# The work ahead of attention in another order: keys and queries first, natural-layout values among the first row maxima, the attention pool in two

## The chip, the core and the metric

The kernel runs on one core of one Trainium2 chip. The metric is the device time of one execution in microseconds (us); it was taken three times for the kernel before. Engines are named as in the profile: PE (TensorE, matmul; PEld is its weight load), DVE (VectorE), ACT (ScalarE), POOL (GpSimd), SP (SyncE, which issues the DMAs).

## What is computed

One transformer layer with a sequence of 1,024 tokens and a width of 1,024, in f32. Only its first third matters here:

```python
h = _rms_norm(x, norm_mix); u = h @ w_in
q, kc, vc, ks, vs, kw, vw, gate_logits, rw, merge = split(u)
# NSA attention, 8 heads of 64, 2 key groups, three branches:
#  c: compress(kc), compress(vc): blocks of 32 tokens at stride 16 -> silu -> 63 keys and values
#  s: 16 selected blocks of 64 (with 16 blocks in all: every causal token)
#  w: a window of 512 tokens
# q and the keys of each branch are rms-normed per head with a gain
o = g_c * attn_c(q) + g_s * attn_s(q) + g_w * attn_w(q)
o_rwkv = rwkv7(rw)            # token mix, low-rank ("lora") projections, a scan, group norm
x = x + (gate0 * (o @ proj_nsa) + gate1 * (o_rwkv @ proj_rwkv)) @ w_out
x = x + conv_ffn(_rms_norm(x, norm_ffn))
```

## The kernel before

Every projection is a product of f32 numbers split in a high and a low part (`hhi`, `hlo` of the normed input; `whi`, `wlo` of a weight). `wload` (L245) loads a weight of 128 output columns, splits it on ACT (L252) and DVE or POOL (L254). `passes` (L293) runs 24 matmuls of 512 columns for each half of the tokens (L264: eight `k` with `whi` by `hhi` and `hlo`, then eight with `wlo`), and calls an evacuation. So a projection of both halves is 48 matmuls.

The PSUM banks have tags: P and B for projections, A for attention scores, M for sums of squares (`RTAG`) and for the row maxima; `psM` has two banks. A scheduler orders the instructions of each engine by a priority that starts with the order of the program text; a wait for a buffer or a value moves nothing past an instruction on the same engine once the order is set.

`rms64` (L362) norms a projection per head: square on ACT (L364), a matmul with ones by blocks (L366), logarithm and exponential on ACT (L368, L369, each in its own table set), a product on DVE (L370). `kstack` (L379) writes the normed keys, as f16 high and low parts, to the stacked layouts `k1*` and `k2*` by six DMAs.

`kphase` (L390) runs once. It compresses keys (`kv` = 0) and then values (`kv` = 1): a projection, copies into `zp`, 32 small matmuls with `cw1` (L429), a SiLU that ends in `hid` (L440), a product with `cw2` (L443 for keys, L452 for values), and for the keys a norm and `kstack`. Then come the values in natural layout (tokens on partitions): one load `wn` of 128 x 2240, split in `wnh` (ACT, L461) and `wnl` (POOL, L462), and for each of eight token groups 24 matmuls of 280 columns into psA (L469), two copies and two differences into `Vs` and `Vw`, and the gates' exponential `gat` (L473 to L475). After that the mask constants `cb` are loaded (L478, into the buffer of `wn`) and cast (L479), and the keys s and w are projected, normed and stacked (L481 to L493).

`attention` (L516) calls `kphase`, opens the pool "attq" where the pool of `kphase` was, and projects the first queries (`qproj(0)`, L499). Then come eight units (four query pairs `i`, two groups `g`). Each loads `qd`, `q2` by DMA (L534 to L536), computes row maxima of branches s and w block by block (L554 and mask L558 into psM, DVE's reduction L560), of branch c (L566), turns them into shifts, and then for each branch and half computes scores (L608 to L612 into psA), two exponentials on ACT (`ph` L617, `pf` L618), a difference on DVE (`pl` L619) and the products with the values (L622 to L627 into psB). The units' written order interleaves the row maxima of the next unit with the exponentials of this one.

Fillers are woven into `attention` by `weave`, one after so many steps, from the list `FO`: numbers are `z` projections (`zproj`, L653; 48 matmuls each and stores to `z_d`), "L" is a step of `loraproj` (its inputs are the stored `z`; four steps j of three products, L980 to L986, evacuated by ACT, L989 and L992, and POOL, into the three buffers "zs" and stored to `lw_d`, `al_d`, `gt_d`, `km_d`). `z` and lora results use the same three "zs" buffers.

## Time and profile before

| | before |
|---|---|
| median of 3 runs | 1774.48 us |
| range of the runs | 1773.18 to 1779.53 us |
| the profiled execution | 1774.76 us |
| its span on the core | 1772.8 us |
| mean granted PE clock | 0.993 |
| matmul records | 11856 |

The profile is one execution. Its page gives the busy time of each engine; the windows view gives it for stretches of the span, in us from the span's start; the view of groups gives count, busy time and mean length in ns by line and shape; the timeline gives the start and length of single instructions, with idle time before them and what ended it in brackets; the view of waits gives, by pair of waiting and awaited instruction, the total in us, how often, and the longest. Matmul lengths include the pipeline, so that the distance of two starts, not the length, is what a matmul costs in a dense stream. L264 is line 264 of the kernel before.

### The profile page before, as it was taken

The page shows a single profiled execution, that of the slowest core. Times are in us where ns is not written, and L with a number is a line of the kernel's source. Part 1 is how long each engine was busy: PE and PEld are TensorE (multiplying, and loading weights), DVE is VectorE, ACT ScalarE, POOL GpSimd, SP SyncE. Part 2 cuts the span into 40 slices and gives each one's busy share as a digit, 9 for nine tenths or more (in the row PEclk, how much of TensorE's full clock was granted, in tenths as well). Part 3 has the DMA queues.
Part 4 walks back from the last instruction along what each step waited for, and adds up shares of the span by engine and source line. Part 5 has one row for each costly group of instructions (what it writes and reads, how often), then busy time and mean ns, then how long its engine had stood idle before and what let it go on. Part 6 is the DMA issues. An engine that isn't in the chain of part 4 may idle for free. (4 is left out here: it accounts for less than half of the span.)

```text
span 1772.8 us, 30784 instructions
## 1 busy us (share of the span) xinstructions
PE 1725.8 (97%) x11856; PEld 1350.3 (76%) x11856; DVE 1247.7 (70%) x2197; ACT 888.5 (50%) x1603; POOL 477.7 (27%) x346
## 2 busy tenths in 40 slices
PE   8998999999999999999999999999999999999998
PEld 5885667776777778887777878787888888888886
DVE  6425676777776548764546585499888888875799
ACT  6455674657656754446545563444444434524330
POOL 0102031110121220010013200112534444757856
PEclk9999999999999999999999999999999999999999
DMA  5325143231344445435445763444222222623302
GB/s 193 109 68 181 39 155 108 88 122 43 112 146 127 140 151 196 145 119 160 146 156 173 255 209 115 147 145 141 78 89 80 81 90 72 242 75 123 131 13 107
DMA packets 124258, 224.65 MB, mean 127 GB/s; under 512 B 16336, under 2 KB 45392, under 8 KB 123856
## 3 DMA queue, kind: packets, MB, share of 16 engines
q1 hardware_dynamic: 124112, 222.69, 38.7%
q8 instruction: 93, 1.52, 0.4%
q14 instruction: 53, 0.43, 0.1%
HBM read 153.86 MB, written 63.96 MB: 123 GB/s over the span
## 5 line engine op out<-in xcount | busy, mean ns | idle before, releaser
L264 PE MATMUL psP<-hhi,whi 128*128 128x512 f32 x560 | 229.0, 409 | 1.2 <-ACT hhi L238 0.6
L264 PE MATMUL psP<-hlo,whi 128*128 128x512 f32 x560 | 225.3, 402 | 0.0
L254 DVE TENSOR_TENSOR wlo<-wraw,whi 128x1024 fp32r<-128x1024 f32 (+1 forms) x98 | 112.0, 1144 | 76.4 <-ACT whi L252 37.4
L619 DVE TENSOR_TENSOR pl<-pf,ph 128x512 f16<-128x512 f32 (+3 forms) x208 | 117.2, 572 | 55.0 <-ACT pf L618 53.8
L264 PE MATMUL psP<-hhi,wlo 128*128 128x512 f32 x560 | 153.7, 403 | 0.0
L252 ACT ACTIVATE whi<-wraw 128x1024 fp32r<-128x1024 f32 (+1 forms) x98 | 93.0, 953 | 92.2 <-PE psP L264 41.5
L617 ACT ACTIVATE ph<-psA 128x512 f16<-128x512 f32 (+3 forms) x208 | 99.4, 478 | 66.9 <-PE psA L612 33.5
L264 PEld LDWEIGHTS psP<-hhi,whi 128*128 128x128 f32 x560 | 105.9, 189 | 26.0 <-DVE zs L659 1.2
L264 PEld LDWEIGHTS psP<-hlo,whi 128*128 128x128 f32 x560 | 105.9, 189 | 23.2 <-issue 1.4
L560 DVE TENSOR_REDUCE mp<-psM 128x1 f32<-128x512 f32 (+1 forms) x192 | 95.1, 515 | 34.9 <-PE psM L558 26.5
L264 PEld LDWEIGHTS psP<-hhi,wlo 128*128 128x128 f32 x560 | 103.0, 188 | 21.6 <-issue 0.5
L1539 POOL TENSOR_TENSOR wlo<-wraw,whi 128x1024 fp32r<-128x1024 f32 (+1 forms) x33 | 64.7, 1960 | 146.5 <-PE psA L264 46.9
L618 ACT ACTIVATE pf<-psA 128x512 f32<-128x512 f32 (+3 forms) x208 | 100.2, 482 | 0.0
L622 PEld LDWEIGHTS <-ph 128*128 128x128 f16 x592 | 55.8, 96 | 18.3 <-issue 7.8
L627 PEld LDWEIGHTS <-pl 128*128 128x128 f16 x592 | 54.9, 98 | 18.7 <-issue 6.1
L1339 POOL TENSOR_TENSOR b<-b,bonus 128x512 f32<-128x512 f32 x8 | 10.4, 1302 | 205.2 <-ACT b L1337 170.2
L641 POOL TENSOR_TENSOR onat<-onat,ot 128x256 f32<-128x256 f32 x32 | 28.3, 891 | 135.0 <-DVE ot L640 119.3
L1539 POOL TENSOR_TENSOR s34l<-s,s34h 128x1024 fp32r<-128x1024 f32 x16 | 39.2, 2450 | 93.2 <-ACT s34h L1538 93.2
L1482 DVE SCALAR_TENSOR_TENSOR th<-th,u 128x512 f32<-128x512 f32 x38 | 59.5, 1566 | 0.1
L625 PEld LDWEIGHTS <-ph 128*128 128x128 f16 x592 | 56.1, 97 | 2.4 <-issue 1.7
L1538 ACT ACTIVATE whi<-wraw 128x1024 fp32r<-128x1024 f32 (+1 forms) x38 | 33.4, 879 | 41.5 <-PE psP L1603 28.7
L1603 PE MATMUL psP<-h2h,whi 128*128 128x512 f32 x128 | 50.8, 397 | 1.2 <-ACT p L1629 1.2
(812 smaller groups left out, 5119.1 us busy)
## 6 DMA issues: line engine op xcount, KB each, us to landing
wraw<-f_up SPq DMA_DIRECT2D x56, 512.0 KB, 3.5
wraw<-w_t SPq DMA_DIRECT2D x46, 512.0 KB, 4.0
wraw<-f_dn SPq DMA_DIRECT2D x22, 512.0 KB, 4.1
th_d<-th SPq DMA_DIRECT2D x38, 256.0 KB, 2.1
sg_d<-zs SPq DMA_DIRECT2D x32, 256.0 KB, 2.4
wraw<-w_out SPq DMA_DIRECT2D x16, 512.0 KB, 3.5
z_d<-zs SPq DMA_DIRECT2D x28, 256.0 KB, 3.7
x<-xT SPq DMA_DIRECT2D x24, 256.0 KB, 5.5
```

The source lines that it names most:

```text
L252: A.activation(hi[:, :nk], raw, AF.Copy)
L254: (V if WK[0] <= wk[0] < WK[1] else G).tensor_sub(lo[:, :nk], raw, hi[:, :nk].bitcast(F32))
L264: lastm[0] = T.matmul(ps, a[:, k], ks_(b, k), start=(n == 0), stop=(n == 3 * nk - 1)).ins
L560: V.reduce_max(mp[:, x, br, t:t + 1], pm[:, 0:(b1 - b0) * 128], axis=AX.X)
L617: A.activation(ph[0:nkey, rg], pa[0:nkey, rg], AF.Exp, scale=0.125)
L618: A.activation(pf[0:nkey, rg], pa[0:nkey, rg], AF.Exp, scale=0.125)
L619: V.tensor_sub(pl[0:nkey, rg], pf[0:nkey, rg], ph[0:nkey, rg])
L622: T.matmul(pov[:, t, :], ph[0:nkey, tk], vt[0:nkey, kb, g, 0:65], start=first, stop=False, skip_group_check=True)
L625: T.matmul(pov[:, t, 0:64], ph[0:nkey, tk], vt[0:nkey, kb, g, 65:129], start=False, stop=False, skip_group_check=True)
L627: T.matmul(pov[:, t, :], pl[0:nkey, tk], vt[0:nkey, kb, g, 0:65], start=False, stop=True, skip_group_check=True)
L1482: V.scalar_tensor_tensor(th, th, 0.5, ub, op0=ALU.mult, op1=ALU.mult)
L1539: e.tensor_sub(lo[:, ks], raw[:, ks], hi[:, ks].bitcast(F32))
```

## The change

All of it is in the order of the work up to the first unit of attention, and in where the buffers lie that this order needs. Line numbers move: `rms64` is at L376 to L384 after, the row maxima's matmul at L580, the natural values' at L512, a projection's at L268, the exponentials at L650 and L651, the z evacuation at L691, the lora evacuations at L1022 and L1025.

- Both compressions run up to `hid` before either product with `cw2`; those products go to psM. The mask constants are loaded first, in four pieces on buffers of the later `prep` pool, and cast on POOL.
- The queries `q0` are projected between keys s and keys w. The norms of keys and `q0` use buffers of the `prep` pool (`ktile`). The lora weights' raw loads use these buffers too, so they are loaded behind.
- The natural-layout values become a function, `vnat`, that is emitted after the row maxima of branch w of the first unit; the matmuls of token group t are held until row maximum number 3t + 1 is issued.
- "attq" is opened first and holds queries, maxima and shifts; the pool of `kphase` is closed behind `vnat`, and a second attention pool "attp" in its place holds `onat`, `pf`, `ph`, `pl`, `cf`, `ot`, `oT`.
- Two z projections (4 and 8) trade places in `FO`.

```diff
+VPA = 3
+VPB = 1
+VAT = (0, 0, 1)
+PKT = "MM"
-FO = (12, 13, "L", 0, "L", 4, "L", 8, "L")
+FO = (12, 13, "L", 0, "L", 8, "L", 4, "L")
...
+        def ktile(x):
+            kr[0] += x == "s"
+            t_ = {"s": ("t1", "cum"), "r": ("e2", "BK"), "n": ("km", "kk")}[x][kr[0] % 2]
+            return prep.tile([128, 512], F32, name="k" + x, tag=t_, bufs=1)
...
+            cl4 = [prep.tile([128, 512], F32, name=f"cl{i}", tag=t_) for i, t_ in enumerate(("km", "kk", "t1", "cum"))]
+            for i in range(4):
...
+                load(cl4[i][:, :w_], D["cst"][:, 256 + 512 * i:256 + 512 * i + w_])
+                G.tensor_scalar(cb[:, 512 * i:512 * i + w_], cl4[i][:, :w_], 1.0, 0.0, op0=ALU.mult, op1=ALU.add)
+            z = tmp.tile([128, 2240], F32, name="zp", tag="wnl")
...
+                hids.append(hid)
+            for kv, hid in enumerate(hids):
+                if kv == 0:
+                    pk = ps(PKT[0])
...
+            for nm, br, wi, gi in (("s", 0, 2, 2), ("w", 1, 3, 3)):
+                if br:
+                    qproj(0, "A", ktile)
...
+        def vnat():
...
+            for t in range(8):
+                pn = ps("A")
...
+                for k in range(8):
+                    with tc.issue_after(pms[min(VPA * t + VPB, len(pms) - 1)]) if k == 0 and VPA else ExitStack():
                         for a, b in ((hhi, wnh), (hlo, wnh), (hhi, wnl)):
                             T.matmul(pn[:, 0:280], a[t // 4][k][:, tk], b[:, k], start=(n == 0), stop=(n == 23))
...
         def attention():
-            yield from kphase()
-            AQ["p"] = pool("attq", 1, stack=ast, side="right")
+            AQ["q"] = pool("attq", 1, stack=ast, side="right")
...
-            qproj(0, "A")
+            kst = ExitStack()
+            AQ["k"] = pool("ktmp", 1, stack=kst, side="right")
+            yield from kphase()
...
+                        if (i, g, br) == VAT:
+                            vnat()
+                            kst.close()
+                            AQ["p"] = pool("attp", 1, stack=ast, side="right")
...
+                    if g == 0:
+                        onat = AQ["p"].tile([128, 8, 128], F32, name="onat", bufs=2)
```

PE at the second compression, before: `hid` is the first compression's result, `zp_343` and `zp_344` the inputs of the convolution, `cw_349` the weight `cw2`.

```order
L264 MATMUL psP<-hhi_92,wlo 128x512
L429 MATMUL psA<-zp_343,cw_347 64x64
L429 MATMUL psA<-zp_344,cw_347 64x64
...
L443 MATMUL psA<-hid,cw_349 128x63
...
L429 MATMUL psA<-zp_343,cw_348 64x64
L429 MATMUL psA<-zp_344,cw_348 64x64
L366 MATMUL psM<-nsq,cst_f 128x63
```

The same place after, with the numbers 365 and 366 for the convolution's weights and 367 for `cw2`.

```order
L268 MATMUL psP<-hhi_107,wlo 128x512
L452 MATMUL psA<-zp,cw_365 64x64
L268 MATMUL psP<-hhi_108,wlo 128x512
L268 MATMUL psP<-hhi_109,wlo 128x512
L452 MATMUL psA<-zp,cw_365 64x64 x15
L452 MATMUL psA<-zp,cw_366 64x64 x16
L468 MATMUL psM<-hid,cw_367 128x63
L268 MATMUL psP<-hhi_110,wlo 128x512
```

The product with `hid` stood inside the second convolution and ahead of most of it; it now stands behind the whole of it, and a projection runs on both sides.

PE at the first row maxima of the first unit, before: `lx` and `llo` are the lora input and weights, `k1s_322` the stacked keys s, `cb` and `identb` the mask and an identity.

```order
L980 MATMUL psP<-lx_2075,lhi_1693 128x512
L986 MATMUL psP<-lx_2075,llo 128x512
L554 LDWEIGHTS qd
L554 MATMUL psM<-k1s_322,qd 128x128
L558 LDWEIGHTS identb
L558 MATMUL psM<-cb,identb 128x128
L554 LDWEIGHTS qd
L554 MATMUL psM<-k1s_322,qd 128x256
```

The same place after: `wnh` and `wnl` are the value weights.

```order
L268 MATMUL psP<-hhi_114,whi 128x512
L580 LDWEIGHTS qd
L580 MATMUL psM<-k1s_322,qd 128x256
L585 LDWEIGHTS identb
L585 MATMUL psM<-cb,identb 128x128
L512 MATMUL psA<-wnh,hhi_107 128x280
L512 MATMUL psA<-wnh,hlo_115 128x280
L512 MATMUL psA<-wnl,hhi_107 128x280
```

What stands between the row maxima was the lora block, two or three matmuls at a time; now it is a z or w projection and then the natural values, 24 matmuls at a time.

ACT where the first unit's exponentials begin, before: `zs` are the lora evacuations, `q_1182` the shifts.

```order
L989 ACTIVATE zs<-psP 128x512
L582 ACTIVATE q_1182<-psM 64x512 x2
L364 ACTIVATE nsq<-psP 128x512
L252 ACTIVATE whi<-wraw 128x1024
L617 ACTIVATE ph<-psA 128x512
L618 ACTIVATE pf<-psA 128x512
L617 ACTIVATE ph<-psA 128x384
L618 ACTIVATE pf<-psA 128x384
```

The same place after:

```order
L518 ACTIVATE gat<-psA 128x24
L1025 ACTIVATE zs<-psP,pd 128x512
L613 ACTIVATE q_941<-psM 64x512 x2
L650 ACTIVATE ph<-psA 128x512
L651 ACTIVATE pf<-psA 128x512
L1022 ACTIVATE zs<-psP 128x512
L650 ACTIVATE ph<-psA 128x384
L651 ACTIVATE pf<-psA 128x384
L1025 ACTIVATE zs<-psP,pd 128x512
```

The lora evacuations, all ahead of the exponentials before, now begin among the last natural values and go on between the exponentials, one after each pair or two.

More of the change, by code (lines that the diff above doesn't have):

```diff
@@ L423, in kphase @@
-                    project(W01[kv], hhi, hlo, 8, ev, tag="PB"[kv])
-                    yield KY[kv]
-                    ph = ps("A")
-                    for l in range(16):
-                        j, c = divmod(l, 8)
-                        for g in range(2):
-                            T.matmul(ph[64 * g:64 * g + 64, j:j + 64], cw1[kv][j][:, c], zp[g][:, c, 2 * j:2 * j + 64],
-                                     start=(l == 0), stop=(l == 15), skip_group_check=True)
-                    cb_ = tmp.tile([128, 1], F32, name="cvb", bufs=2)
@@ new lines, in kphase @@
+                project(W01[kv], hhi, hlo, 8, ev, tag="PB"[kv])
+                yield KY[kv]
+                ph = ps("A")
+                for l in range(16):
+                    j, c = divmod(l, 8)
+                    for g in range(2):
+                        T.matmul(ph[64 * g:64 * g + 64, j:j + 64], cw1[kv][j][:, c], zp[g][:, c, 2 * j:2 * j + 64],
+                                 start=(l == 0), stop=(l == 15), skip_group_check=True)
+                cb_ = tmp.tile([128, 1], F32, name="cvb", bufs=2)
@@ new lines, in kphase @@
+                hids.append(hid)
+            for kv, hid in enumerate(hids):
+                if kv == 0:
+                    pk = ps(PKT[0])
+                    T.matmul(pk[:, 0:63], cw2[:, 0], hid, start=True, stop=True)
+                    rms64(pk[:, 0:63], 63, P("gain", 1), kcn[:, 0:63], ktile)
+                    kch = tmp.tile([128, 128], F16, name="kch")
+                    kcl = tmp.tile([128, 128], F16, name="kcl")
+                    V.tensor_copy(kch, kcn)
+                    V.tensor_sub(kcl, kcn, kch)
+                    kstack("c", 2, kch, kcl)
+                else:
+                    pv = ps(PKT[1])
+                    T.matmul(pv[0:63, 0:128], hid, cw2[:, 1], start=True, stop=True)
+                    src = pv[0:63, 0:128].rearrange("p (g d) -> p g d", g=2)
+                    A.activation(Vc[0:63, 0, :, 0:64], src, AF.Copy)
+                    V.tensor_sub(Vc[0:63, 0, :, 65:129], src, Vc[0:63, 0, :, 0:64])
@@ new lines, in kphase, with ev @@
+            for nm, br, wi, gi in (("s", 0, 2, 2), ("w", 1, 3, 3)):
+                if br:
+                    qproj(0, "A", ktile)
+                kh = tmp.tile([128, S], F16, name="kh")
+                kl = tmp.tile([128, S], F16, name="kl")
+                def ev(h, pj):
+                    kn = ktile("n")
+                    rms64(pj, 512, P("gain", gi), kn, ktile)
+                    A.activation(kh[:, H[h]], kn, AF.Copy)
+                    V.tensor_sub(kl[:, H[h]], kn, kh[:, H[h]])
+                project(WT[wi], hhi, hlo, 8, ev, tag="PB"[br])
+                kstack(nm, br, kh, kl)
+                yield KY[2 + br]
```

171 lines of the change are left out of this document (73 added, 98 removed).

## Prediction

> **What bounds the kernel now.** I read the page first, for what the kernel as a whole is short of.
>
> ```profile
> span 1772.8 us, 30784 instructions
> ...
> PE 1725.8 (97%) x11856; PEld 1350.3 (76%) x11856; DVE 1247.7 (70%) x2197; ACT 888.5 (50%) x1603; POOL 477.7 (27%) x346
> ```
>
> TensorE (PE) is busy for 97% of the span. The change keeps all matrix products and only moves some, so it can gain only where PE stands still or trickles. The move ends early: in the written order of PE the two kernels meet again at about the 1118th matmul of some 10,300, inside the first unit's exponential part, and run in practically the same order from there. In the trace of before that point lies at 216 us. So the question is how much earlier or later PE comes to that point; behind it PE is busy nearly all the time, and what is won there should last to the end.
>
> Next I asked the windows view for the stretches before that point: busy time per engine (with counts), then the granted PE clock, the DMA share and GB/s.
>
> ```profile
> core 0: us, PE busy (x) PEld busy (x) DVE busy (x) ACT busy (x) POOL busy (x), PEclk, DMA share, GB/s
> 50.00:66.00 16.00, 13.77 (x161) 11.47 (x160) 12.16 (x17) 5.19 (x14) 8.40 (x6) 0.90 0.39 128
> 66.00:150.00 84.00, 84.00 (x445) 71.05 (x444) 25.40 (x51) 48.06 (x81) 1.95 (x4) 1.00 0.26 75
> 150.00:177.00 27.00, 20.60 (x94) 11.18 (x93) 16.31 (x34) 9.75 (x16) 7.61 (x13) 0.91 0.64 208
> 177.00:190.00 13.00, 13.00 (x64) 10.09 (x62) 1.76 (x6) 4.60 (x8) 0.75 (x1) 0.93 0.28 96
> 190.00:216.00 26.00, 23.04 (x307) 15.30 (x307) 22.73 (x55) 20.57 (x49) 0.96 (x1) 1.00 0.07 21
> ```
>
> The stretches are: the two compressions (50 to 66), natural-layout values with keys and queries (66 to 150, without a gap), the row maxima (150 to 177), one z projection alone (177 to 190), and the exponentials (190 to 216). The hole is 150:177: only 94 matmuls in 27 us. "Busy" flatters it, since a lone matmul is shown with its whole latency. So I counted that stretch by form and priced each at the spacing of dense streams.
>
> ```profile
> L980 PE MATMUL psP<-lx,lhi 128*128 128x512 f32 x12 | 6.1, 508 | 3.0 <-ACT zs L992 2.0 <-ACT zs L989 1.0
> L558 PE MATMUL psM<-cb,identb 128*128 128x128 bf16 x20 | 4.2, 228 | 0.0
> L986 PE MATMUL psP<-lx,llo 64*128 64x512 f32 x8 | 4.1, 508 | 0.0
> L554 PE MATMUL psM<-k1s,qd 128*128 128x512 f16 x6 | 2.6, 463 | 0.6 <-DVE mp L560 0.6
> L983 PE MATMUL psP<-lx,llg 128*128 128x512 f32 x4 | 2.1, 514 | 0.0
> L982 PE MATMUL psP<-lxl,lhi 128*128 128x512 f32 x4 | 2.1, 513 | 0.0
> L264 PE MATMUL psP<-hhi,wlo 128*128 128x512 f32 x8 | 2.0, 389 | 0.0
> L554 PE MATMUL psM<-k1w,qd 128*128 128x512 f16 x5 | 1.8, 385 | 0.7 <-DVE mp L560 0.7
> ```
>
> The timeline gives the spacings (start, length): f32 matmuls of 512 columns follow each other by 0.23 us, f16 ones by 0.21, masks of 128 columns by 0.06 (188.80 to 188.86). It also shows where the low-rank (lora) block begins and where dense work resumes.
>
> ```profile
> 151.77 0.40 PE L980 MATMUL psP<-lx,lhi 128*128 128x512 f32 x1
> ...
> 153.92 0.22 PE L554 MATMUL psM<-k1s,qd 128*128 128x128 f16 x1 [1.34 <-DMA qd<-qh]
> ...
> 176.53 0.63 PE L264 MATMUL psP<-hhi,whi 128*128 128x512 f32 x1
> ...
> 179.03 0.39 PE L264 MATMUL psP<-hhi,whi 128*128 128x512 f32 x1
> 179.26 0.40 PE L264 MATMUL psP<-hlo,whi 128*128 128x512 f32 x1
> ...
> 188.80 0.22 PE L558 MATMUL psM<-cb,identb 128*128 128x128 bf16 x1
> 188.86 0.27 PE L554 MATMUL psM<-k1s,qd 128*128 128x256 f16 x1
> ...
> 192.19 0.38 PE L608 MATMUL psA<-qd,k1s 128*128 128x512 f16 x1
> 192.40 0.38 PE L610 MATMUL psA<-q,k2s 128*128 128x512 f16 x1
> ```
>
> The 36 f32 matmuls of the rows above are 36 x 0.23 = 8.3 us, the 11 large f16 ones 2.3, the 20 masks 1.2. The 27 smaller ones that are left are, by my estimate from the same spacings, about 2.4. So 14.2 us of streaming take 27: **12.8 us are lost** there. The view of waits says to what.
>
> ```profile
> ACT zs L992 <- DMA km_d<-zs: 5.1, 3, 2.9
> ...
> ACT zs L989 <- DMA z_d<-zs: 3.1, 1, 3.1
> ...
> ACT zs L989 <- DMA lw_d<-zs: 2.1, 1, 2.1
> PE psM L554 <- DVE mp L560: 2.0, 4, 0.7
> ```
>
> The row maxima wait for DVE's reductions, which give the two banks of psM back. The only work written between them is the lora block, and that goes at the pace at which its three "zs" buffers are stored: 5.1 + 3.1 + 2.1 = 10.3 us of waiting on ACT. Its four steps last from 151.77 to 176.53, 6.2 us each.
>
> **The change part by part.** All sums are against the profiled execution, 1774.76 us (span 1772.8, some 2 us around it), which lies 0.3 us above the median of 1774.48.
>
> *Compressions.* Before, the second one waits for the first one's `hid`:
>
> ```profile
> 50.35 4.97 POOL L462 TENSOR_TENSOR wnl<-wn,wnh 128x2240 fp32r<-128x2240 f32 x1 [7.55 <-ACT wnh L461]
> ...
> 51.67 4.93 DVE L947 TENSOR_TENSOR llo<-lraw,lhi 64x512 fp32r<-64x512 f32 x2 [4.62 <-PE psA L429]
> ...
> 62.27 0.43 PE L443 MATMUL psA<-hid,cw 128*128 128x63 f32 x2 [1.72 <-DVE hid L440]
> ```
>
> In 50:66 PE idles 16.00 - 13.77 = 2.2 us, and the clock of 0.90 costs up to another 1.4: 3.6 in all. The change issues both convolutions before the small product that needs `hid`, and the lora weights (L947) leave this place. I take 3.0 of the 3.6; none of it is the low end.
>
> The POOL row has a sequel. The split of the value weights (4.97 us) now waits until the compressions have left a buffer that it shares, so it falls beside the splits of key and query weights on DVE. In the rows above DVE's pair began under POOL's operation and ended 1.3 us after it, at 56.60; so the first of the two stood nearly until POOL's end at 55.32. PE needs such a split only 16 matmuls (16 x 0.23 = 3.7 us) into a half, so a delay of 4.97 shows as 1.3 at most; some of it should be covered. I put +0.5, from 0 to +1.3. The Trainium skill, "SBUF — State Buffer", section "Who interferes with whom", says that a VectorE operation with two SBUF inputs and a GpSimd operation that reads SBUF lock each other out for a whole instruction. The trace agrees (one of 51.67 until 55.32); it is a rule against the change, with that same 1.3 as its price.
>
> *Keys and queries.* In 66:150 the 192 natural-value matmuls covered the norms of the compressed and the selected keys. That cover is gone: behind the compressions only the projections are left. This is the chain of one half, with two table loads in it; the last two rows are a weight split and the square that begins each chain.
>
> ```profile
> 144.93 1.28 ACT L368 ACT_TABLE_LOAD   x1
> 146.22 0.69 ACT L368 ACTIVATE nrs<-psM,epst 128x512 f32<-128x512 f32 x1
> 146.93 1.28 ACT L369 ACT_TABLE_LOAD   x1
> 148.22 0.63 ACT L369 ACTIVATE nrs<-nrs 128x512 f32<-128x512 f32 x1
> ...
> 149.85 0.62 ACT L510 ACTIVATE qh<-qn 128x512 f16<-128x512 f32 x1
> ...
> 148.89 0.75 DVE L370 SCALAR_TENSOR_TENSOR qn<-psA,par,nrs 128x512 f32<-128x512 f32 x1 [2.99 <-ACT nrs L369]
> ...
> L252 ACT ACTIVATE whi<-wraw 128x1024 fp32r<-128x1024 f32 x4 | 4.2, 1050 | 3.0 <-DMA k1s<-kl 3.0
> ...
> L364 ACT ACTIVATE nsq<-psA 128x512 f32<-128x512 f32 x2 | 1.2, 588 | 4.8 <-DMA k2w<-kh 4.8
> ```
>
> Square 0.59, sum on PE about 0.5, load 1.28, logarithm 0.69, load 1.28, exponential 0.63, DVE 0.75, cast 0.62: 6.3 us, 5.1 of it on ACT. There are seven such norms: the compressed keys and two halves each of s, q0 and w. That is 7 x 5.1 = 36 us on ACT, and with weight splits and the rest about 50 by my count of the written order, against some 54 of PE work from there to the first row maximum. So it is tight but fits. Following the order by hand with these durations I find two new stalls: about 1.3 us where q0's weight split stands on ACT behind a key square, and about 2.6 us where the first reduction stands on DVE behind w's second half, whose load, logarithm, load, exponential (3.9) end later, while PE has about 1.3 us of other work. **+3.9**, from 0 (all covered) to +17 (the chains run one after another; below).
>
> The Trainium skill, "ScalarE: Activation LUTs", section "What ACT_TABLE_LOAD costs", gives about 1283 ns for a load and about 1380 ns more of draining for every switch of sets. The trace has the load (1.28) and not the drain: 146.22 + 0.69 = 146.91, and the next load starts at 146.93. By the page, fourteen loads would put about 19 us more on ACT, which would bring the slower rival.
>
> *Row maxima.* They now start at about 105 us in my walk, with 192 matmuls of natural values between them, eight groups of 24, each held behind a row maximum, so the old 12.8 us have cover. The new filler isn't free of ACT and DVE either: each token group needs three evacuations on ACT and two on DVE, in turns with the reductions. I put **-12.8 and +1.5** (0 to +6). The half clock at 177:190 goes with its cause: 13 x 0.07 = **-0.9**. The Trainium skill, "TensorE: Matmul & The Clock Gate", Part 1, has the clock halve after a window of some 3.4 us that is idle; the trace shows the low means (0.90, 0.91, 0.93) only in and right behind the trickling stretches, and 1.00 elsewhere.
>
> *Exponentials of the first unit.* Now the 48 z matmuls that ran alone (48 x 0.23 = 11 us) and three of the four lora steps fall in here. The matmuls fill holes: before, 26.00 - 23.04 = 3.0 us of plain idle plus trickle. The lora steps bring their waits for stores onto ACT, which is in order and already 20.57 of 26 us busy. I take 0 for the two together, from -4 to +6.
>
> *At no cost:* the swap of two z projections in the filler order (equal sizes), constants cast in four pieces (POOL idles there), the second pool (names and places), two more table loads (1.28 each, ACT idles half the time). Their cover is ACT and POOL slack; without it 2.6 us.
>
> Sum: -3.0 + 0.5 + 3.9 - 12.8 + 1.5 - 0.9 + 0 = **-10.8 us**, so 1774.76 - 10.8 = **1764.0 us**.
>
> **The rivals.**
>
> *Paid back in the exponentials.* Three lora steps at 6.2 us are 18.6 us there. If the 10.3 us of store waits return, three quarters of them (7.7) before exponentials that PE waits for, the gain falls to about 3: **1771.7**. For it: ACT's order, and three buffers still. Against: z matmuls are cover. Chance 0.24.
>
> *More than I take.* The stalls of 3.9 and 0.5 are covered and the z matmuls fill 2 us of the exponentials' holes: 10.8 + 6.4 = 17.2, so **1757.6**. For it: 66:150 ran without a gap. Against: that cover has moved. Chance 0.16.
>
> *Slower: ACT strings the norms.* If the seven chains don't overlap, they take 7 x 6.3 = 44 us from 62, four weight splits (1.05 each) and the z and lora casts some 7, and the copies of the queries about 4: the first row maximum comes at 62 + 44 + 4 + 7 + 4 = 121 instead of 105. The natural values can't fill that hole, as they are held behind the row maxima. That is 16 us of idle, and the lowered clock that comes with such holes (16 x 0.10 = 1.6 in 50:66, 27 x 0.09 = 2.4 in 150:177) adds 4: -10.8 + 20 = +9, **1784**. It decides when the first row maximum comes later than 105 + 10.8 = 116 us; from there the change loses. For it: the cover is gone. Against: psP, psA and psB take different halves, so squares and sums run ahead, and the trace packs ACT without gaps (146.91 to 146.93). Chance 0.12.
>
> That the values aren't interleaved at all can be excluded: the written order of PE has them between the row maxima.
>
> **How the numbers follow.** My forecast has 0.48, the rivals 0.24, 0.16 and 0.12. The term bounds alone give about 1757 to 1772; the range reaches from the better rival into the first one and on towards the slower one, which it leaves out in its larger half: 1756 to 1776. Half a per cent, 8.9 us, is about what a measurement of this kernel can tell from no change: faster means under 1765.6, slower over 1783.4. Of the forecast's 0.48 I count 0.40 below 1765.6, with the better rival's 0.16 and 0.02 of the first: faster 0.58. The slower rival lies about its bound and its tail goes beyond 1784; with other mishaps I put 0.11 there. The rest, 0.31, is within.
>
> **What would show it.** Right: PE without waits for `hid`; the first row maximum at 103 to 109 us; PE clock near 1.00 from there to the exponentials; the first unit's exponentials starting near 157 instead of 188; the meeting point at 205 instead of 216; equal times behind it. Wrong, if the first row maximum comes after 116, if ACT's waits for `km_d` and `lw_d` stores reappear between exponentials with PE waiting for `ph`, or if what is won at the meeting point is gone later.

## The result, and the profile after

The changed kernel takes 1760.82 us (median of 5, 1757.66 to 1765.52) beside 1776.47 us for the kernel before (median of 5): a ratio of 0.9916, 95% interval 0.9893 to 0.9938. A second set of runs gave 1761.15 beside 1773.68, ratio 0.9928 (0.9903 to 0.9952). So it is faster by 12 to 16 us; the forecast was 1764.0 with 1756 to 1776.

The profiled execution of the changed kernel took 1757.66 us, the quickest of its five. Its page:

```profile
span 1755.7 us, 30772 instructions
...
PE 1716.0 (98%) x11856; PEld 1341.3 (76%) x11856; DVE 1250.2 (71%) x2197; ACT 891.4 (51%) x1605; POOL 480.2 (27%) x349
```

The span is 17.1 us shorter, PE's busy time 9.8. The windows view of the early part shows where (compressions, keys and queries, first row maxima, natural values between the row maxima, last of them, first unit's exponentials; columns as before, the PE clock third from the end):

```profile
50.00:66.00 16.00, 16.00 (x177) 12.70 (x176) 6.03 (x14) 6.70 (x16) 2.52 (x5) 1.00 0.22 74
66.00:105.00 39.00, 39.00 (x163) 29.98 (x162) 17.01 (x22) 30.23 (x37) 3.32 (x1) 1.00 0.30 78
105.00:130.00 25.00, 21.01 (x119) 16.90 (x118) 11.03 (x21) 14.01 (x25) 0.00 (x0) 1.00 0.54 147
130.00:157.00 27.00, 26.91 (x177) 22.92 (x176) 14.92 (x34) 8.35 (x23) 0.62 (x1) 1.00 0.21 66
157.00:180.00 23.00, 22.81 (x180) 14.79 (x179) 15.45 (x38) 16.34 (x37) 8.37 (x12) 1.00 0.57 197
180.00:205.00 25.00, 23.67 (x255) 17.05 (x254) 14.21 (x33) 14.61 (x32) 1.59 (x2) 1.00 0.16 55
```

The old hole (94 matmuls in 27 us at a clock of 0.91) is gone: 130:157 holds 177 matmuls at 1.00. One new and smaller hole stands at 105:130, with 4.0 us of idle PE. The view of waits, PE from 45 to 212 us, names it:

```profile
PE psM L580 <- DVE mp L587: 2.5, 1, 2.5
PE psM L580 <- ACT kr L382: 1.5, 1, 1.5
PE psB L655 <- ACT ph L650: 1.1, 2, 0.9
PE psM L597 <- ACT qr L382: 0.8, 1, 0.8
```

A row maximum waits 1.5 us for a bank of psM that the sum of squares of w's second half still holds, until ACT has taken its logarithm. The next waits 2.5 us because a reduction stands on DVE behind that half's product. Ahead of that logarithm ACT itself stands 2.38 us for the load of the low-rank weights `lrawg`, whose buffer the key norms now use: the load is issued at 108.4, when the product of w's first half (107.60 to 108.35) has read that buffer. The timeline shows the chain (start, length, in brackets the idle time before):

```profile
111.40 0.63 ACT L981 ACTIVATE lhi<-lrawg 128x512 fp32r<-128x512 f32 x1 [2.38 <-DMA lrawg<-lora]
...
112.05 1.28 ACT L382 ACT_TABLE_LOAD   x1
...
113.34 0.69 ACT L382 ACTIVATE kr<-psM,epst 128x512 f32<-128x512 f32 x1
...
114.08 0.27 PE L580 MATMUL psM<-k1s,qd 128*128 128x256 f16 x1 [1.53 <-ACT kr L382]
...
116.59 0.75 DVE L384 SCALAR_TENSOR_TENSOR kn<-psB,par,kr 128x512 f32<-128x512 f32 x1 [1.20 <-ACT kr L383]
...
118.64 0.88 DVE L587 TENSOR_REDUCE mp<-psM 128x1 f32<-128x384 f32 x2
...
119.24 0.38 PE L580 MATMUL psM<-k1s,qd 128*128 128x512 f16 x1 [2.46 <-DVE mp L587]
```

To compare kernels I use moments that all of them have (starts in the profiled executions, in us): the first and the 24th row maximum matmul of the first unit, its first exponential `ph`, and the 1,300th matmul record, which lies just behind the meeting point and is the same matmul in every kernel whose PE order meets the others' there.

| | before | changed | shift |
|---|---|---|---|
| first row maximum | 153.9 | 106.2 | -47.7 |
| 24th row maximum | 172.0 | 162.0 | -10.0 |
| first exponential | 188.7 | 167.1 | -21.6 |
| first exponential of the second unit | 228.3 | 218.6 | -9.7 |
| matmul 1,300 | 229.1 | 219.4 | -9.7 |
| matmul 2,000 | 313.1 | 300.6 | -12.5 |
| last exponential of attention | 641.2 | 629.3 | -11.9 |
| last matmul | 1768.4 | 1751.3 | -17.1 |

The 21.6 us at the first exponential shrink to 9.7 one unit later: the 48 z matmuls that ran alone before (11 us) now run among the exponentials. They were moved, not saved.

**The clock is part of it.** Each execution has its mean granted PE clock, and the spread inside one kernel is mostly this: of 26 executions of the kernel before, those at 0.993 took 1768.4 to 1773.2 us, the one at 0.998 took 1763.2, the one at 0.988 took 1778.2. One thousandth of a span of 1,772 us is 1.77 us. So below I also give the time less span x (1 - mean clock), "at full clock"; the clock is given to 0.001, so this is good to about 1 us. By the trace's record of the clock it drops to one half for windows of 3.41 us, each worth up to 1.7 us. Before has three of them ahead of the meeting point (62.9, 161.9 and 175.5 us), the changed kernel's profiled execution none. The Trainium skill, "TensorE: Matmul & The Clock Gate", Part 1, gives a window of the same length, 3413 ns.

### The profile page after: what moved, and what is told of

Read it like the earlier page. It is cut to its first block, busy times and chain, and to the rows that moved or that the text cites. A ratio compares the mean times of both kernels' runs of the same rounds, so it can differ in the third digit from the quotient of the medians.

```text
span 1755.7 us, 30772 instructions
## 1 busy us (share of the span) xinstructions
PE 1716.0 (98%) x11856; PEld 1341.3 (76%) x11856; DVE 1250.2 (71%) x2197; ACT 891.4 (51%) x1605; POOL 480.2 (27%) x349
## 5 line engine op out<-in xcount | busy, mean ns | idle before, releaser
L268 PE MATMUL psP<-hhi,whi 128*128 128x512 f32 x560 | 227.7, 407 | 0.9 <-DVE zs L692 0.6
L268 PE MATMUL psP<-hlo,whi 128*128 128x512 f32 x560 | 225.4, 402 | 1.7 <-DVE hlo L243 1.7
L268 PE MATMUL psP<-hhi,wlo 128*128 128x512 f32 x560 | 154.4, 404 | 0.0
L650 ACT ACTIVATE ph<-psA 128x512 f16<-128x512 f32 (+3 forms) x208 | 99.4, 478 | 73.2 <-PE psA L645 43.8
L268 PEld LDWEIGHTS psP<-hlo,whi 128*128 128x128 f32 x560 | 105.5, 188 | 24.8 <-DVE hlo L243 2.7
L268 PEld LDWEIGHTS psP<-hhi,whi 128*128 128x128 f32 x560 | 105.4, 188 | 24.8 <-DVE zs L692 1.4
L268 PEld LDWEIGHTS psP<-hhi,wlo 128*128 128x128 f32 x560 | 102.4, 188 | 21.3 <-issue 0.5
L587 DVE TENSOR_REDUCE mp<-psM 128x1 f32<-128x512 f32 (+2 forms) x192 | 95.9, 516 | 31.4 <-PE psM L585 25.0
L651 ACT ACTIVATE pf<-psA 128x512 f32<-128x512 f32 (+3 forms) x208 | 100.0, 481 | 0.0
```

The source lines that it names most:

```text
L268: lastm[0] = T.matmul(ps, a[:, k], ks_(b, k), start=(n == 0), stop=(n == 3 * nk - 1)).ins
L587: V.reduce_max(mp[:, x, br, t:t + 1], pm[:, 0:(b1 - b0) * 128], axis=AX.X)
L650: A.activation(ph[0:nkey, rg], pa[0:nkey, rg], AF.Exp, scale=0.125)
L651: A.activation(pf[0:nkey, rg], pa[0:nkey, rg], AF.Exp, scale=0.125)
```

## The experiments

"Undone" means in the changed kernel, the rest as changed. Ratios are against the kernel before, run beside on the same chip. Behind the first set of the changed kernel there are three, each on a chip of its own (e1 to e4, e5 to e8, e9 to e12); at full clock the kernel before agrees between the second and the third and is 2.3 us lower in the first, so times at full clock are compared with care across them. Where the scheduler left PE's written order behind the meeting point as it was, the whole time can be read; where not, only the early moments can.

| | median us | ratio, 95% | median clock | at full clock | first row max. | 24th | first exp. | matmul 1,300 |
|---|---|---|---|---|---|---|---|---|
| before, three sets (26, 9, 9 runs) | 1771.9, 1773.7, 1773.0 | | 0.993, 0.993, 0.994 | 1759.6, 1761.9, 1761.9 | 153.9 | 172.0 | 188.7 | 229.1 |
| changed, first set | 1760.8 | 0.9916 (0.9893 to 0.9938) | 0.996 | 1754.0 | 106.2 | 162.0 | 167.1 | 219.4 |
| e1 values ahead of keys | 1769.7 | 0.9991 (0.9976 to 1.0005) | 0.993 | 1756.8 | 132.0 | 171.5 | 177.7 | 229.5 |
| e2 before, fourth buffer | 1786.9 | 1.0082 (1.0054 to 1.011) | 0.989 | 1764.9 | 154.1 | 173.6 | 190.9 | order differs |
| e3 before, compressions alone | 1770.4 | 0.9985 (0.9965 to 1.0005) | 0.994 | 1760.0 | 152.6 | 171.9 | 187.0 | 229.1 |
| e4 filler order undone | 1762.2 | 0.9953 (0.9932 to 0.9973) | 0.994 | 1754.0 | 105.9 | 161.4 | 166.5 | 218.9 |
| e5 changed, again | 1761.2 | 0.9928 (0.9903 to 0.9952) | 0.996 | 1753.4 | 106.4 | 163.3 | 168.4 | 220.7 |
| e6 mask constants late | 1755.3 | 0.9902 (0.9878 to 0.9927) | 0.998 | 1751.1 | 104.7 | 161.2 | 166.4 | 218.8 |
| e7 sums of w in psA | 1792.9 | 1.0109 (1.0084 to 1.0135) | 0.988 | 1770.8 | 105.3 | 158.5 | 168.7 | order differs |
| e8 values not held | 1790.6 | 1.0091 (1.0062 to 1.012) | 0.986 | 1766.8 | 105.0 | 161.0 | 168.0 | order differs |
| e9 compressions undone | 1761.5 | 0.993 (0.9911 to 0.9948) | 0.997 | 1755.4 | 108.7 | 164.3 | 169.4 | 221.7 |
| e10 queries behind w | 1765.4 | 0.9953 (0.9931 to 0.9974) | 0.994 | 1754.8 | 124.8 | 166.3 | 180.1 | 222.4 |
| e11 e6, released at 3t | 1764.1 | 0.9949 (0.9929 to 0.9969) | 0.996 | 1758.5 | 104.1 | 164.0 | 168.6 | 222.4 |
| e12 e6, released at 4t + 1 | 1761.0 | 0.9925 (0.9908 to 0.9943) | 0.996 | 1753.4 | 104.3 | 157.9 | 169.1 | 219.1 |

### e1: are the values as cover the gain?

```diff
-VPA = 3
+VPA = 0
+            vnat()
             for nm, br, wi, gi in (("s", 0, 2, 2), ("w", 1, 3, 3)):
...
-                            vnat()
                             kst.close()
```

> The changed kernel with one thing undone: the natural-layout values stand ahead of the keys again instead of between the first unit's row maxima; compressions, queries before w, pools and filler order stay as changed. Theory A (the values as cover for the row maxima are most of the gain): a stretch like the old 150 to 177 us returns, with the low-rank block alone between the row maxima; PE loses 9 to 13 us there and the time is 1769 to 1775 us, 3 to 7 below the kernel before (1776.5). Rival B (the gain comes from the earlier queries and the compressions, and the interleaving only moves work): the time stays within 3 us of the changed kernel's 1760.8.

Measured: 1769.7 us, and matmul 1,300 at 229.5, where before had it (229.1). All of the gain up to there is gone, although the row maxima start 22 us earlier than before. The windows of this kernel show the hole back, clock included:

```profile
105.00:132.00 27.00, 27.00 (x113) 20.59 (x112) 7.99 (x11) 19.08 (x25) 0.00 (x0) 1.00 0.34 79
132.00:150.00 18.00, 16.21 (x76) 11.96 (x76) 8.56 (x15) 8.57 (x12) 0.00 (x0) 1.00 0.56 164
150.00:171.00 21.00, 14.73 (x56) 7.55 (x55) 13.69 (x26) 9.63 (x17) 3.99 (x6) 0.84 0.53 176
```

Only 56 matmuls run in 150:171, with the clock at 0.84. Theory A stands. The ratio's interval takes in 1: without the interleaving the rest of the change is not shown to gain anything in time (at full clock 1756.8 for 1759.6). Part of what the interleaving gains is the clock: the trace of e1 has three half-clock windows ahead of matmul 1,300 (two from 156.5 us on, one at 214.5; up to 5.1 us together), the changed kernel's none. At full clock e1 is 2.8 us above e4, the kernel of its set that lies nearest to the changed one.

### e2: does the ring of three buffers pace the old hole?

```diff
-                                t2 = FP["f"].tile([128, 512], F32, name="zs", bufs=NZS)
+                                t2 = FP["f"].tile([128, 512], F32, name="sq0", tag="sq0")
```

> The kernel before with a fourth buffer for the low-rank results (the product that goes to km_d gets one of its own), nothing else. Theory A (the hole at the row maxima is paced by the stores of the three buffers, 10.3 us of ACT waits): those waits fall by half or more, the stretch from 150 to 177 us shortens by 4 to 8 us, and the time falls to 1769 to 1773 us. Rival B (the hole is paced by the row maxima themselves, their two PSUM banks and the reductions on DVE): the stretch shortens by under 2 us and the time stays at 1774 to 1777 us.

ACT's waits in 150 to 182 us have other stores in them now:

```profile
ACT zs L992 <- PE psP L986: 6.0, 4, 3.1
...
ACT zs L992 <- DMA al_d<-zs: 4.7, 1, 4.7
...
ACT zs L989 <- DMA lw_d<-zs: 2.6, 1, 2.6
```

The wait for km_d (5.1 us before) is gone, but the row maxima take 173.6 - 154.1 = 19.5 us against 18.1. So theory A falls: taking one store's wait away doesn't shorten the hole, and waits for other stores and for PE itself come up. The scheduler also reordered PE as a whole (in the traces, 7,124 of the 10,656 matmul records behind the 1,200th differ from those of before), so the 1786.9 us say nothing on the ring, and rival B isn't shown by this either. What paced the old hole beyond "no other work" stays open.

### e3: the compressions alone, in the kernel before

```diff
+                    hids.append(hid)
+                for kv, hid in enumerate(hids):
                     if kv == 0:
                         pk = ps("A")
```

> The kernel before with the compressions alone as in the change: both convolutions up to hid before either product with cw2. Theory A: the wait of 1.7 us for hid goes and with it the half clock at about 63 us; everything behind comes 2.5 to 3.5 us earlier and the time is 1773 to 1774 us. Rival B: the low-rank weights' split on DVE stays beside the split of the value weights on POOL, so what PE gains at the first product it loses at the second, and the meeting point moves by under 1 us.

Ratio 0.9985, with 1 inside. PE is 1.7 us ahead up to the 1,200th matmul and level at the 1,250th; this execution has a half-clock window at 213.9 us between the two. Of the 1.7 us, 0.6 are there at the 150th matmul already, ahead of the compressions' products, where the two kernels are the same. The product with `hid` still finds PE idle for 1.0 us (1.7 before), and then the natural values (L472 in this kernel) wait for a bank of psA until the norm of the compressed keys has read it:

```profile
PE psA L472 <- DVE kcn L370: 2.3, 1, 2.3
```

Neither theory in its size: about 1 us, less than half of what was expected, and no gain that the time shows.

### e4: the two z projections back

```diff
-FO = (12, 13, "L", 0, "L", 8, "L", 4, "L")
+FO = (12, 13, "L", 0, "L", 4, "L", 8, "L")
```

> The changed kernel with the filler order of before (z projection 4 ahead of 8). Theory A (equal sizes, no effect): the same time within 1.5 us at every place, 1759 to 1763 us. Rival B (the 2.8 us that the changed kernel gains between 216 and 310 us, in the second low-rank step, come from the swap): the meeting point stays where it is and PE is 2 to 3 us later from about 300 us on, 1762 to 1765 us.

1762.2 us, 1754.0 at full clock as the changed kernel; against the changed kernel's trace PE is 0.6 us earlier at matmul 1,300 and 0.4 later at matmul 2,000. In the time this is theory A: the swap is worth nothing that shows. But not at every place: from matmul 1,300 to 2,000 the changed kernel takes 81.2 us in both of its traces (e6, e9, e10 and e12 too), e4 82.1 and before 84.0. So 1.0 of the 2.8 us that the changed kernel gains there goes with the swap; at the last exponential of attention e4 is 0.3 us ahead again. Before, PE also has waits there that after has not (waits of PE, before in 216 to 330 us):

```profile
PE psP L980 <- ACT zs L992: 1.1, 2, 0.6
PE psM L580 <- DVE Mt L576: 0.6, 1, 0.6
PE psB L627 <- DVE pl L619: 0.2, 1, 0.2
PE psP L980 <- ACT zs L989: 0.2, 1, 0.2
```

They come to 2.1 us, 1.3 of them for low-rank evacuations (L980); why the second low-rank step runs smoother wasn't tried.

### e5: the changed kernel again, for the clock

No edit.

> The changed kernel, unchanged, again beside the kernel before on this chip, so that each run's granted clock can be set against its time. Theory A (about half of the gain is idle PE that is filled, and the other half is half-clock windows of 3.41 us that no longer follow the hole at the row maxima): at equal mean clock the two kernels differ by 5 to 7 us, and the changed kernel's mean clock is higher by 0.002 to 0.004, worth 1.77 us for each 0.001. Rival B (the clock differs from run to run by chance and not by kernel): the mean clocks of the two agree within 0.001, and the gain here is 5 to 7 us in all.

Six executions: median clock 0.996 beside 0.993 for the kernel before, 1753.4 beside 1761.9 at full clock. So some 8 us are PE's own time and some 5 the clock (7.0 us lost to it against 12.4). That is theory A in kind, with a larger own part (8.5 for the 5 to 7 expected; among e1 to e4, e4 is 5.6 us below before at full clock). But the clock is chance too. The profiled execution here is at 0.992 and has half-clock windows in the scan where the first one has none; here 826 to 886 us, changed kernel first, then again:

```profile
826.00:886.00 60.00, 58.25 (x732) 47.49 (x727) 32.04 (x69) 32.11 (x61) 5.21 (x4) 1.00 0.49 160
```

```profile
826.00:886.00 60.00, 55.95 (x653) 44.98 (x651) 28.57 (x60) 28.74 (x54) 5.16 (x4) 0.89 0.46 150
```

The same instructions in the same order: 732 matmuls in one, 653 in the other, and the later execution falls back 7.7 us between matmuls 7,000 and 7,500. So of the 17.1 us between the two first profiles, the 5 that arise in the scan (matmuls 7,400 to 8,000) can't be put down to the change; before has three half-clock windows from 837 to 933 us, the changed kernel one. The early windows go with the hole: before, e1 and e3 have windows between 156 and 215 us, two or three of 3.41 us each. The profiled executions of the changed kernel and its variants with the same tail (e4, e5, e6, e9, e10, e12) have at most one, at 117 to 122 us in the new hole; e11, whose row maxima ran short of cover, has two.

### e6: the mask constants later

```diff
-            cl4 = [prep.tile(..., tag=t_) for i, t_ in enumerate(("km", "kk", "t1", "cum"))]
+            cl4 = [prep.tile(..., tag=t_) for i, t_ in enumerate(("zk", "lw", "zr", "al"))]
...
             for kv, hid in enumerate(hids):
```

The whole block of loads and casts stands behind the first loop over `kv`; the new buffers are those of the compressions' weights, so that the loads wait until these are read.

> The changed kernel with the mask constants' four pieces loaded into the buffers of the compression weights, so that the casts on POOL come after the compressions and not beside the splits of the normed input on DVE at 20 to 25 us. Theory A (the 1.1 us that the changed kernel loses at 26 to 28 us come from DVE standing behind POOL there): PE is 1.0 to 1.2 us earlier from 30 us on, and the time falls by about 1, to 1758 to 1761 us. Rival B (PE's wait there has another cause, the later weights on the DMA queue): no change at 30 us.

In the changed kernel the casts fall beside the splits of the normed input (POOL, DVE, PE of its timeline):

```profile
20.33 4.06 POOL L413 TENSOR_SCALAR cb<-cl 128x512 bf16<-128x512 f32 x4 [18.26 <-DMA cl<-cst]
...
22.82 1.09 DVE L243 TENSOR_TENSOR hlo<-hf,hhi 128x512 fp32r<-128x512 f32 x1
...
26.78 0.50 PE L268 MATMUL psP<-hlo,whi 128*128 128x512 f32 x1 [0.95 <-DVE hlo L243]
```

With the constants late the same split takes 0.69 and a cast 0.62:

```profile
22.15 0.69 DVE L243 TENSOR_TENSOR hlo<-hf,hhi 128x512 fp32r<-128x512 f32 x1
...
57.59 0.62 POOL L464 TENSOR_SCALAR cb<-cl 128x512 bf16<-128x512 f32 x1 [3.94 <-DMA cl<-cst]
```

PE is 1.2 us earlier at the 50th matmul than in the first trace of the changed kernel and 1.4 than in the second (which also has a window in the new hole), and at matmul 1,300 it is 0.7 and 2.0 earlier. In all eight traces with the early casts the 50th matmul starts at 26.8 to 27.8 us, in the six without (before, e2, e3, e6, e11, e12) at 25.5 to 26.4. PE's wait there is for DVE, not for a load, which rules out rival B. The time is 1755.3 us, ratio 0.9902 (0.9878 to 0.9927), the lowest of all kernels here; at full clock 1751.1, 2.3 below the changed kernel. Theory A, with a time below the 1758 to 1761 that it gave. That it beats the changed kernel as well is likely but not proved by the ratios, whose intervals overlap; the share of the clock in the 5.9 us between the two medians may be chance.

### e7 and e8: the new hole, and the hold on the values

```diff
-            pss = ps(RTAG)
+            pss = ps(tg)
...
-                    rms64(pj, 512, P("gain", gi), kn, ktile)
+                    rms64(pj, 512, P("gain", gi), kn, ktile, "MA"[br])
```

> The changed kernel with the sums of squares of the keys w in psA instead of psM, the two banks that the row maxima use. Theory A (the new hole of 4 us at 112 to 119 us is a row maximum that waits for the bank of a sum, 1.5 us behind the logarithm on ACT, and for a reduction behind w's product on DVE, 2.5): the hole shrinks to under 2 us, PE comes 2 to 3 us earlier to the meeting point and the time is 1757 to 1760 us. Rival B (the first unit's start is set by ACT's chain and not by PE): the hole goes, but PE waits later, and the meeting point stays within 1 us.

```diff
-VPA = 3
+VPA = 0
```

> The changed kernel with the natural-layout values' groups not held behind numbered row maxima; the scheduler places them by priority and readiness, first of them before the second row maximum. Theory A (any dense work between the row maxima serves as cover): the values fill the hole at 112 to 119 us, and what they no longer cover later costs about as much; the time is within 2 us of the changed kernel. Rival B (the pace of one group for three row maxima is what keeps DVE and ACT level): the values are used up early, the last row maxima run with the low-rank block alone, PE loses 3 to 6 us there, and the time is 1763 to 1767 us.

Both are some 30 us slower than the changed kernel, and neither theory spoke of that. The place is not here. Attention ends nearly as before: the last exponential starts at 631.1 and 630.7 us against 629.3. The loss comes behind it, in the scan. The small edit had the scheduler write PE's order anew behind the meeting point (in the traces, about half of the 10,656 matmul records behind the 1,200th differ from the changed kernel's). The scan, 770 to 910 us, in e7 and then in the changed kernel:

```profile
770.00:840.00 70.00, 66.33 (x794) 54.29 (x793) 33.90 (x75) 33.62 (x60) 5.12 (x4) 0.88 0.42 129
840.00:910.00 70.00, 62.66 (x767) 50.65 (x767) 30.79 (x67) 32.12 (x60) 5.12 (x4) 0.85 0.40 124
```

```profile
770.00:840.00 70.00, 65.81 (x904) 53.93 (x903) 37.38 (x81) 43.65 (x77) 5.65 (x4) 1.00 0.46 148
840.00:910.00 70.00, 68.64 (x831) 55.92 (x830) 33.92 (x71) 34.99 (x67) 5.83 (x5) 0.98 0.40 131
```

The clock is at 0.88 and 0.85 there, which alone makes 70 x (0.12 + 0.13) = 17.5 us against the changed kernel; another 6.8 us are longer waits on the scan's own chain, from 630 to 1,000 us:

```profile
PE psC L1143 <- DVE yc L1364: 9.0, 6, 3.5
```

(2.2 us in the changed kernel.) Where the remaining 10 us or so go stays open. What the experiments asked can be read from the early moments alone. In e7 PE waits 5.5 us for reductions (100 to 235 us), where the changed kernel waits 2.5 for one and 1.5 for the logarithm; the 24th row maximum is 3.5 us earlier and the first exponential 1.5 later. Theory A fails on the latter and B isn't shown; it is inconclusive. In e8 the values fill half of the hole (PE 6.07 us busy from 112 to 120, against 4.01), the low-rank block is left alone behind them, and the second unit's first exponential is 3.6 us later than in the changed kernel: rival B's direction, 222.2 against 218.6.

From here on, kernels were chosen whose PE order behind the meeting point stays as it was.

### e9: the compressions undone

```diff
-                hids.append(hid)
-            for kv, hid in enumerate(hids):
-                if kv == 0:
+                hids.append(hid)
+                if kv == 0:
```

> The changed kernel with the compressions alone undone: each product with cw2 right behind its own convolution. PE's written order behind the meeting point is that of the changed kernel to the last matmul, so what is lost early stays. Theory A (the second convolution no longer waits for hid, worth 3 us by the prediction): the wait of 1.5 to 2 us returns at about 60 us, the first row maximum comes 2 to 4 us later, and the time adjusted for the granted clock (time minus the half-clock loss) is 2 to 4 us above the changed kernel's 1753.5. Rival B (as in the kernel before with the compressions alone, where 1 us came of it): under 1.5 us at the first row maximum and in the adjusted time.

The first row maximum is 2.5 us later, matmul 1,300 2.3, the time at full clock 2.0 (1755.4 against 1753.4). Against e5, whose trace has a half-clock window in the new hole as e9's has, matmul 1,300 is 1.0 later. That is A's size at the first row maximum and less behind it, and without A's reason: the product with `hid` doesn't wait at all here (first row). PE waits at the next norm instead, for a square on ACT. That stands behind the SiLU of the second compression, which waits for DVE, and DVE stands in a cast until POOL's split of the value weights ends at 69.61 us (the rows are from the timelines of PE, POOL, DVE and ACT):

```profile
61.62 0.43 PE L467 MATMUL psM<-hid,cw 128*128 128x63 f32 x2
...
64.59 5.03 POOL L503 TENSOR_TENSOR wnl<-wn,wnh 128x2240 fp32r<-128x2240 f32 x1 [10.04 <-PE psA L452]
...
67.23 2.46 DVE L471 CAST kch<-kcn 128x128 f16<-128x128 f32 x1
...
69.92 0.26 ACT L460 ACTIVATE th<-hid 128x63 f32<-128x63 f32 x1 [2.53 <-DVE hid L458]
...
70.72 1.13 PE L380 MATMUL psM<-ks,cst_f 128*128 128x512 f32 x2 [1.57 <-ACT ks L378]
```

In the kernel before the same cast takes 0.22 us.

### e10: queries behind w

```diff
-                if br:
-                    qproj(0, "A", ktile)
...
                 kstack(nm, br, kh, kl)
+                if br:
+                    qproj(0, "A", ktile)
                 yield KY[2 + br]
```

> The changed kernel with the queries q0 projected behind the keys w instead of ahead of them; PE's written order behind the meeting point is unchanged. Theory A (queries ahead of w hide the DMA to qd under w's projection): the first row maximum comes later by one projection, 48 x 0.23 = 11 us, at 115 to 119 us, and since the natural values still fill the row maxima, most of it is only moved; the meeting point comes 1 to 4 us later. Rival B (the place of the queries is worth nothing, the norms on ACT set the pace): within 1 us.

The first row maximum comes at 124.8 (18.6 later), matmul 1,300 at 222.4 (2.9 later; 1.6 later than in e5, whose trace has a half-clock window as this one has), 1765.4 us. That is theory A's size at the meeting point, but neither its 11 us at the first row maximum nor its reason: PE doesn't wait for the DMA to `qd`. It stands before the row maxima for a bank of psP that ACT has not yet emptied (`zlast`, at 117.54), and ACT has the logarithm (114.43) and the exponential (117.00) of the queries' second half ahead of that:

```profile
117.75 0.80 PE L268 MATMUL psP<-hhi,whi 128*128 128x512 f32 x1 [4.08 <-ACT zlast L695]
```

### e11 and e12: the pace of the values

Both edits are made in e6's kernel.

```diff
-VPB = 1
+VPB = 0
```

> The kernel of the late mask constants with the natural values released one row maximum earlier (3t instead of 3t + 1). PE's written order behind the meeting point is practically the same. Theory A (the hole at 112 to 119 us is PE without a matmul that may run): the hole shrinks by 1 to 3 us and the time is 1752 to 1755 us. Rival B: the values run out earlier and the last row maxima wait instead; no change within 1 us.

```diff
-VPA = 3
+VPA = 4
```

> The kernel of the late mask constants with the natural values spread wider (released at row maximum 4t + 1 instead of 3t + 1). PE's written order behind the meeting point is the same to the last matmul. Theory A (24 matmuls, 3.1 us, cover three row maxima and not four): the row maxima take longer, PE loses 2 to 5 us more between 106 and 162 us, and the time is 1757 to 1762 us. Rival B (the reductions set the pace in any case): no change within 1 us of 1755.3.

e11: against e6, matmul 1,300 is 3.6 us later and the time 1764.1 (1758.5 at full clock). Releasing the values earlier makes it slower: PE waits 3.0 us for reductions and 2.5 for the logarithm, and 122:162, nearly full in the changed kernel, has 37.26 of 40 us at a clock of 0.96.

```profile
122.00:162.00 40.00, 37.26 (x228) 31.25 (x227) 19.31 (x43) 12.06 (x32) 0.62 (x1) 0.96 0.21 62
```

Both theories fall; the values run short. e12: the 24th row maximum comes 3.3 us earlier than in e6, matmul 1,300 0.4 later, 1753.4 at full clock against 1751.1. In the early part that is nearer to B: the row maxima don't take longer, and 4t + 1 costs 0.4 us at the meeting point. The time, 1761.0 us, is within A's range and outside B's 1 us; of the 5.7 us to e6, 2.3 are left at full clock, little more than its rounding. So neither theory is shown.

## Why the prediction was right, and where its steps were off

- **Direction and mechanism: right; the size in part by luck.** The row maxima of the first unit lacked other work; the values are that work. The terms "-12.8 and +1.5" for it, 11.3 us, measure 10.0 in e1 (matmul 1,300 back from 219.4 to 229.5), half-clock windows included, and 8.8 against e5. The meeting point was forecast 10.8 us earlier and is 9.7 (8.4 by e5). That the sum comes so near is luck in part: it has a loss too large (next point), a cost at nothing (the casts) and a clock too small; the first two make the gain smaller than the sum, the third makes it larger.
- **"14.2 us of streaming take 27: 12.8 us are lost": mis-sized.** The sum priced all f32 matmuls at 0.23 us, but those of the low-rank block lie further apart, in the old hole and in the changed kernel alike (PE, before and then changed):

```profile
155.75 0.47 PE L980 MATMUL psP<-lx,lhi 128*128 128x512 f32 x1
156.15 0.50 PE L986 MATMUL psP<-lx,llo 64*128 64x512 f32 x1
156.58 0.55 PE L554 MATMUL psM<-k1s,qd 128*128 128x512 f16 x2
```

```profile
174.35 0.58 PE L1013 MATMUL psP<-lx,lhi 128*128 128x512 f32 x1
174.86 0.50 PE L1019 MATMUL psP<-lx,llo 64*128 64x512 f32 x1
175.29 0.20 PE L660 MATMUL psB<-Vs,pl 128*128 128x65 f16 x1
```

  The distances are 0.40 and 0.43 us before, 0.51 and 0.43 after. In the changed kernel the block's 28 matmuls take 10.3 us by the distance of starts (150 to 182 us, clock 1.00), not 28 x 0.23 = 6.4. These 3.9 us come with the block wherever it runs, so the old hole lost about 8.9 and not 12.8. The windows view gives the same: 27.00 - 20.60 = 6.4 of idle PE and 27 x 0.09 = 2.4 of clock, 8.8 together. "Busy" flattered the stretch much less than the prediction held.
- **The clock: mis-sized.** The prediction had the half clock as -0.9 beside what lay inside the 12.8. In the time it is more: 0.993 against 0.996 in the mean, some 5 of the 13 us or so. Part of that is the three early windows (one at the compressions, two in the hole), which are gone, and part is the scan's, which come and go between executions of one kernel.
- **"At no cost: constants cast in four pieces (POOL idles there)": the step that failed.** POOL does idle there, but the cover named was the wrong engine's: DVE's splits stand behind POOL's casts, and PE behind DVE. It costs 1.1 us by the first trace and 1.2 to 1.4 by e6. The prediction weighed the same contention for the value weights and not here. The Trainium skill, "SBUF — State Buffer", section "Who interferes with whom", holds for this place as well, and the trace agrees (1.09 beside a cast, 0.69 alone).
- **The value weights' split: right that PE is spared.** DVE stands for 5.01 us behind POOL there (below), but no weight split was due.
- **New stalls of 3.9: right in sum, half right in place.** 1.5 + 2.5 = 4.0 us. The reduction behind w's second half is as foreseen (2.6 forecast). The other 1.3 were put to q0's weights behind a square; that didn't happen, and a bank of psM held by a sum cost 1.5 instead. Ahead of both stands a wait that no term had: ACT's 2.38 us for the low-rank weights, 2.0 to 2.5 in e4 to e7 and e9 to e12 as well. Whether the two stalls go when that load is moved wasn't tried; in e8, where it is 0.27 us, the hole is half as long, but the values run there too.
- **Compressions, -3.0: about right where they stand, smaller behind, and the reason incomplete.** The stretch 50:66 is full at a clock of 1.00, so the 3.6 us of idle and clock are gone from it. e9 puts 2.5 us on the order of the products at the first row maximum, 1.0 to 2.3 at matmul 1,300 and 2.0 in the time at full clock; e3, in the old surroundings, about 1. In e9 the wait for `hid` doesn't come back: what decides is which operation of DVE falls beside POOL's split of the value weights. In the changed kernel that is one that PE doesn't wait for, in e9 a cast in the chain of the compressions.
- **Queries ahead of w** had no term of their own; e10 puts 2.9 us on them, 1.6 against e5. The three undone parts add up to 10.0 + 2.3 + 2.9 = 15.2 for 9.7 gained against the first trace of the changed kernel, and to 8.8 + 1.0 + 1.6 = 11.4 for 8.4 against e5: they overlap, and how much of that is the clock windows isn't shown.
- **First row maximum at 105 (103 to 109): 106.2. First exponential near 157: 167.1, wrong.** I left too much work behind the first exponential; the sum up to the meeting point doesn't hang on where this line falls.
- **Exponentials, 0 net: borne out.** PE waits 1.1 us there for `ph`, as before (1.1), with the z matmuls and low-rank steps inside. The rival of being paid back there did not come.
- **The slower rival** needed a first row maximum after 116 us; ACT packed the chains as assumed (30.23 of 39 us busy in 66:105, PE 39.00 of 39.00). The Trainium skill, "ScalarE: Activation LUTs", section "What ACT_TABLE_LOAD costs", adds draining to every switch to another table set, which would have spoken for this rival. The trace doesn't show it: a load is again 1.28 us here, with an activation ahead of it until 112.03 and one at its end (112.05 + 1.28 = 113.33, next at 113.34).
- **"Equal times behind": not quite.** Another 2.8 us come up to matmul 2,000, 1.0 of them with the swap that the prediction put at nothing (e4), and the profiled pair differs by 5 more in the scan, which can't be put down to the change (e5).

## What to carry to other kernels

Look for the stretch with few instructions and give it dense work that nothing waits for yet, at a pace that lasts to its end: the same values released a little earlier (e11) or not held at all (e8) ran short. Under a global scheduler a small edit can rewrite work far behind it (e2, e7, e8: 15 to 32 us slower); compare the written orders first, and judge an edit by moments near it. An engine that idles is not free when its operation holds up another engine's, so a cost of nothing needs the neighbour's name too.

## What the runs showed of the hardware

- In these traces an operation on DVE with two inputs in SBUF stands while POOL runs one that reads SBUF, and so does a cast with one input (2.46 us in e9, 0.22 alone). The longest case, POOL and then DVE in the changed kernel:

```profile
64.17 5.15 POOL L504 TENSOR_TENSOR wnl<-wn,wnh 128x2240 fp32r<-128x2240 f32 x1 [9.02 <-ACT cvb L455]
```

```profile
63.75 0.69 DVE L1008 TENSOR_TENSOR lx<-lx,lx 64x512 fp32r<-64x512 f32 x1 [4.71 <-ACT lx L1003]
...
64.85 5.01 DVE L1008 TENSOR_TENSOR lx<-lx,lx 64x512 fp32r<-64x512 f32 x1
```

  The same operation takes 0.69 us alone and 5.01 beside POOL, ending 0.5 us after it. It slows POOL too: four casts take 4.06 us beside DVE and 0.62 each, 2.5 in all, without.
- The granted clock explains most of the spread between executions of one kernel: 1763.2 us at 0.998 to 1778.2 at 0.988, for the same program.
